# Per-layer embedding by whole fp32 products: weights loaded once, as they are

## The chip, the cores and the metric

The kernel runs on one core of one Trainium2 chip. The metric is the time of one execution in microseconds on the device; for the kernel before, three runs gave a median of 3856.39 us (3851.83 to 3856.41). Profiles and traces are of one further execution.

The engines are named as the profile names them: PE is TensorE (matmuls; PEld its weight loads), DVE is VectorE, ACT is ScalarE, POOL is GpSimd, SP is SyncE, which here only issues DMAs.

## The reference

One layer on 1024 tokens of width 1024, in fp32. What matters here is its end: the product-key experts and the per-layer input embedding.

```python
x = x + peer_ffn(rms_norm(x, norm_ffn[i]), peer_w_q[i], peer_sub_keys[i], peer_u[i], peer_v[i])
x = x + jax.nn.sigmoid(rms_norm(x, norm_ple[i]) @ ple_w_gate[i]) * (p[i] @ ple_w_proj[i])
return rms_norm(x, norm_final)
```

`peer_ffn` selects for every token 8 x 16 = 128 of 16384 experts, each a row `u` and a row `v` of 1024. The token's gates are multiplied by `gelu(h . u)` of the selected rows, and the sum of the `v` rows with these factors is added to x. The embedding multiplies the normed x (1024 wide) by `ple_w_gate` (1024 x 1024) and the input p (256 wide) by `ple_w_proj` (256 x 1024).

## The kernel before

The 1024 tokens are eight blocks of 128, one token per partition. The first part of the kernel (projections, time mixing, attention, selection of experts) takes some 2540 us and is not touched. What follows runs in overlap:

- `gather` (L895 to L909), for each block: the block's normed input is loaded by SP into one buffer, `gh` (L900); 128 times POOL gathers one `u` row per token by an indirect DMA (L904) and the DVE multiplies it with gh and sums it (L906). The rows have seven buffers, shared with `add_rows`. At 2543 us blocks 6 and 7 are still to be gathered, and the selection of the last blocks (L828 to L880, small DVE operations) is not finished.
- `dense` (L972 to L1006), for blocks 0 to 4: the sum over all experts. The factors, spread over all 16384 experts, lie in DRAM as W. SP loads pieces of W (`wr`, L986) and of v (`vr`, L996), both whole fp32. ACT writes a rounded copy as fp32r, the high half (L280), and the DVE the rest, the low half (L282). TensorE multiplies high by high, high by low and low by high (L1000 to L1002), and the DVE adds each finished bank to x (L1005).
- `add_rows` (L912 to L922), for blocks 5, 6 and 7: POOL gathers `v` rows (L919) and the DVE adds each with its factor (L921). Block 7's x lies in the buffer `gh`, so that its rows read `gh<-u,gate,gh`. They are the last rows of the kernel, and 93 of these 128 follow after the dense sum's last add.
- `ple_weights` and `ple`: the per-layer embedding and the final norm of all eight blocks, in the order 0 to 7. For a block, p and the normed x (`h`, L1042) are transposed by TensorE (L252), copied to SBUF by ACT as fp32r high halves (L257 for h, L255 for p), and the DVE makes low halves (L263, L261). The gate product has 8 steps over k for each of two halves n of the columns, the product with p 2 steps: 20 products of 128 x 128 by 128 x 512 a block, each as three fp32r matmuls (L292 to L294). ACT takes the sigmoid (L1052), the DVE multiplies (L1055), adds to x (L1057) and, after a norm, scales by gf (L1059); SP stores (L1060).
- `ple_weights` splits the weights in the same manner: each slice of 128 x 512 is loaded into one of two buffers `raw` (L1019), ACT makes the high half (L280), the low half is made by the DVE and POOL by turns (L282). Eight slices (w_pg, n = 0) lie in the right-hand pool and are loaded while the dense sum runs; the other twelve (w_pg, n = 1, and w_pp) are put into the left-hand pool, into the room that the dense sum leaves, and so come after it.

The order on each engine is set when the program is built: the instructions are placed by a simulated timeline and by priorities (`everything`, its list of steps with a number each; a smaller number goes first). On the chip each engine then works through its instructions in that order and waits on semaphores. SP's queue holds all direct loads and stores, the weights among them, in that order too.

## Time and profile before

| | before |
|---|---|
| median of 3 runs | 3856.39 us |
| profiled execution | 3855.49 us |
| its span (first to last instruction) | 3853.7 us |
| mean granted TensorE clock | 0.888 of full speed |
| busy over the span: PE, DVE, ACT, POOL | 81%, 81%, 32%, 48% |
| opening of the dense sum | 2543 to 2660 us |
| main part of it | 2660 to 3560 us |
| last add of the dense sum (L1005) to the end of the last row (L921) | 3634.3 to 3816.4 us |
| tail (rest of blocks 6 and 7) | 3816.4 to 3853.7 us |

The profile tells for every instruction when it ran, on which engine and by which line of the code, and what ended the idle time before it. An engine with a busy share near 100% in a stretch bounds that stretch if its work is needed there; a share over the whole span says little, since stretches differ. The granted clock is TensorE's, 1.0 being 2.4 GHz and 0.5 being 1.2 GHz. A matmul row's duration is longer than its share of the engine, since matmuls overlap: the step from one start to the next is what one costs. The same holds, by less, for the DVE.

### The profile page before, as it was taken

The page shows a single profiled execution, that of the slowest core. Times are in us where ns is not written, and L with a number is a line of the kernel's source. Part 1 is how long each engine was busy: PE and PEld are TensorE (multiplying, and loading weights), DVE is VectorE, ACT ScalarE, POOL GpSimd, SP SyncE. Part 2 cuts the span into 40 slices and gives each one's busy share as a digit, 9 for nine tenths or more (in the row PEclk, how much of TensorE's full clock was granted, in tenths as well). Part 3 has the DMA queues.
Part 4 walks back from the last instruction along what each step waited for, and adds up shares of the span by engine and source line. Part 5 has one row for each costly group of instructions (what it writes and reads, how often), then busy time and mean ns, then how long its engine had stood idle before and what let it go on. Part 6 is the DMA issues. An engine that isn't in the chain of part 4 may idle for free.

```text
span 3853.7 us, 61140 instructions
## 1 busy us (share of the span) xinstructions
PE 3104.5 (81%) x21615; PEld 2506.3 (65%) x21615; DVE 3110.8 (81%) x7003; ACT 1243.0 (32%) x2682; POOL 1856.3 (48%) x1494
## 2 busy tenths in 40 slices
PE   8998778787978686797866789648888989899767
PEld 7885777775667574577734567536666767677645
DVE  2532788767798786789878868989989999999997
ACT  3221322143121175212126866722222222222233
POOL 0000455544534553553455423346766766666772
PEclk9998899898989796898977789769999999989988
DMA  6236598899979898997988999889999999999984
GB/s 204 88 116 197 169 336 306 302 306 302 335 238 345 294 311 289 311 339 265 334 276 281 306 323 338 295 308 350 382 358 386 378 383 362 375 372 364 347 314 158
DMA packets 502322, 1160.41 MB, mean 301 GB/s; under 512 B 54016, under 2 KB 228352, under 8 KB 502016
## 3 DMA queue, kind: packets, MB, share of 16 engines
q0 software_dynamic: 202752, 738.29, 53.8%
q1 hardware_dynamic: 281984, 402.48, 30.6%
q10 hardware_dynamic: 17280, 15.74, 1.2%
q8 instruction: 171, 2.80, 0.3%
q14 instruction: 135, 1.11, 0.1%
HBM read 1071.38 MB, written 84.93 MB: 300 GB/s over the span
## 4 chain that ended last, share of the span: by engine, by line
PE 25%; DVE 23%; issue 20%; DMA 17%; POOL 9%; ACT 4%; SPq 1%; POOLq 0%; DVEq 0%; ACTq 0%; another core or an unknown queue 0%
DMA u<-in_u_dram,idx 9%; PE mm L290 9%; DVE u L906 8%; POOL u L904 6%; POOL u L919 3%; PE mm L785 2%; PE acc L1001 2%; DVE oa L963 2%; PE acc L1002 1%; DVE gh L921 1%; PE acc L1000 1%; DMA gate<-zT 1%; DMA raw<-zT 1%; PE w L965 1%; DVE x L921 1%
## 5 line engine op out<-in xcount | busy, mean ns | idle before, releaser
L904 POOL DMA_INDIRECT u<-in_u_dram,idx x1024 | 1248.3, 1219 | 1284.3 <-DVE dots L906 681.8
L906 DVE CUSTOM_DVE_ANT_0 u<-u,gh 128x1024 f32<-128x1024 f32 x1024 | 1249.9, 1233 | 220.0 <-DMA u<-in_u_dram,idx 201.8
L919 POOL DMA_INDIRECT u<-in_v_dram,idx x384 | 493.2, 1284 | 246.9 <-DVE x L921 116.4
L1001 PE MATMUL acc<-vlo,Whi 128*128 128x512 f32 x1280 | 529.2, 413 | 74.8 <-DVE vlo L282 73.0
L290 PE MATMUL mm<-hT,w 128*128 128x128 f32 x4608 | 561.4, 282 | 11.5 <-DMA w<-in_w_in_dram 2.3
L290 PEld LDWEIGHTS mm<-hT,w 128*128 128x128 f32 x4608 | 544.7, 197 | 27.7 <-issue 8.8
L1002 PE MATMUL acc<-vhi,Wlo 128*128 128x512 f32 x1280 | 521.1, 407 | 0.0
L1000 PE MATMUL acc<-vhi,Whi 128*128 128x512 f32 x1280 | 373.6, 404 | 90.8 <-DMA vr<-in_v_dram 38.9
L1000 PEld LDWEIGHTS acc<-vhi,Whi 128*128 128x128 f32 x1280 | 247.2, 194 | 167.0 <-ACT vhi L280 84.4
L1001 PEld LDWEIGHTS acc<-vlo,Whi 128*128 128x128 f32 x1280 | 253.0, 198 | 154.3 <-DVE vlo L282 99.1
L290 PE MATMUL mm<-act,w 128*128 128x256 f32 x1280 | 313.6, 399 | 33.5 <-DVE gate L776 14.6
L921 DVE SCALAR_TENSOR_TENSOR x<-u,gate,x 128x1024 f32<-128x1024 f32 x256 | 328.2, 1282 | 8.8 <-DMA u<-in_v_dram,idx 4.6
L280 ACT ACTIVATE vhi<-vr 128x512 fp32r<-128x512 f32 x256 | 158.3, 628 | 513.5 <-DMA vr<-in_v_dram 354.6
L965 PE MATMUL w<-ob,oa 128*128 128x128 f32 x1280 | 221.7, 330 | 96.0 <-ACT ob L959 62.5
L290 PEld LDWEIGHTS mm<-act,w 128*128 128x128 f32 x1280 | 247.8, 200 | 73.8 <-issue 16.9
L1002 PEld LDWEIGHTS acc<-vhi,Wlo 128*128 128x128 f32 x1280 | 253.6, 198 | 53.1
L965 PEld LDWEIGHTS w<-ob,oa 128*128 128x128 f32 x1280 | 202.2, 237 | 120.5 <-ACT ob L959 81.7
L963 DVE TENSOR_SCALAR oa<-cst,pt 128x128 f32<-128x128 f32 x640 | 190.2, 354 | 47.4 <-PE w L965 44.0
L958 ACT ACTIVATE ob<-cst,pt 128x128 f32<-128x128 f32 x640 | 204.0, 394 | 0.1
L280 ACT ACTIVATE Whi<-wr 128x1280 fp32r<-128x1280 f32 x64 | 81.4, 1274 | 313.0 <-PE acc L1001 276.3
L282 DVE TENSOR_TENSOR vlo<-vr,vhi 128x512 fp32r<-128x512 f32 x256 | 175.3, 697 | 5.1 <-ACT vhi L280 5.1
L921 DVE SCALAR_TENSOR_TENSOR gh<-u,gate,gh 128x1024 f32<-128x1024 f32 x128 | 169.9, 1327 | 1.0
(331 smaller groups left out, 4673.7 us busy)
## 6 DMA issues: line engine op xcount, KB each, us to landing
w<-in_w_in_dram SPq DMA_DIRECT2D x144, 512.0 KB
vr<-in_v_dram SPq DMA_DIRECT2D x256, 256.0 KB
W<-ws SPq DMA_DIRECT2D x40, 1024.0 KB
wr<-W SPq DMA_DIRECT2D x64, 640.0 KB
w<-in_w_q_dram SPq DMA_DIRECT2D x64, 512.0 KB
w<-in_w_out_dram SPq DMA_DIRECT2D x32, 512.0 KB
u<-in_u_dram,idx POOLq DMA_INDIRECT x1024
x<-in_x_dram SPq DMA_DIRECT2D x16, 512.0 KB
```

What stands on the lines that cost most here:

```text
L280: self.nc.scalar.activation(act[0], x, AF.Copy)
L290: mm(ps, w[0][:, i], a[0][:, i], start=first, stop=last)
L904: nc.gpsimd.indirect_dma_start(out=u[:], out_offset=None, in_=self.I["u"], in_offset=bass.IndirectOffsetOnAxis(ap=idx[:, k:k + 1], axis=0))
L906: nc.vector.tensor_tensor_reduce(out=u[:], in0=u[:], in1=h[:], scale=1.0, scalar=0.0, op0=OP.mult, op1=OP.add, accum_out=dots[:, k:k + 1])
L919: nc.gpsimd.indirect_dma_start(out=v[:], out_offset=None, in_=self.I["v"], in_offset=bass.IndirectOffsetOnAxis(ap=idx[:, k:k + 1], axis=0))
L921: nc.vector.scalar_tensor_tensor(x, v, gate[:, k:k + 1], x, op0=OP.mult, op1=OP.add)
L958: nc.scalar.activation(c[:, i], self.c("iota"), AF.Abs, bias=pt[:, 1, k + i:k + i + 1])
L963: nc.vector.tensor_scalar(a, self.c("iota"), pt[:, 0, k:k + 1], pt[:, 2, k:k + 1], op0=OP.is_equal, op1=OP.mult)
L965: nc.tensor.matmul(ps[:, i], a, c[:, i], start=True, stop=True)
L1000: nc.tensor.matmul(acc[b], wh, vh, start=i == 0, stop=False)
L1001: nc.tensor.matmul(acc[b], wh, vl, start=False, stop=False)
L1002: nc.tensor.matmul(acc[b], wl, vh, start=False, stop=i == G - 1)
```

## The change

All weights of the embedding are loaded as they are, in fp32, by two DMAs: w_pg (1024 x 1024, 4.19 MB) and w_pp (256 x 1024, 1.05 MB), both into the right-hand pool. The splits of the weights are gone, the second call of `ple_weights` too. Of h and p, ACT makes one whole fp32 copy after the transposes; their low halves are gone. `mm` is not changed: given one part of each factor it issues one matmul per product (L290), and given fp32 on both sides TensorE multiplies whole fp32. Before, an operand was given as two fp32r parts (`R` in the code), now as one fp32 part (`F`).

```diff
-    def ple_weights(self, n, side):
-
-        nc = self.nc
+    def ple_weights(self, side):
         pool = self.pool(self.ctx, "pw", side)
-        if n == 0:
-            self.raw = pool
-        for name, k, n in ([("w_pg", 8, 0)] if n == 0 else [("w_pg", 8, 1), ("w_pp", 2, 0), ("w_pp", 2, 1)]):
-            w = [self.tile(pool, [128, k, 512], R, f"{name}{n}{x}", 1) for x in ("hi", "lo")]
-            for i in range(k):
-                raw = self.tile(self.raw, [128, 512], F, "raw", 2)
-                nc.sync.dma_start(raw, self.I[name][i * 128:i * 128 + 128, n * 512:n * 512 + 512])
-                self.split_to([x[:, i] for x in w], raw, nc.gpsimd if i % 2 else nc.vector)
-            self.pw[name, n] = w
+        for name, k in (("w_pg", 8), ("w_pp", 2)):
+            w = self.tile(pool, [128, k, D], F, name, 1)
+            self.nc.sync.dma_start(w, self.I[name].rearrange("(k p) n -> p k n", p=128))
+            for n in range(2):
+                self.pw[name, n] = (w[:, :, n * 512:n * 512 + 512],)
 ...
-            pair = lambda k, tag: [t([128, k, 128], tag + x, HB, R) for x in ("hi", "lo")]
+            whole = lambda k, tag: [t([128, k, 128], tag + "T", HB)]
 ...
-                hT, pT = pair(8, "h"), pair(2, "p")
+                hT, pT = whole(8, "h"), whole(2, "p")
 ...
-            (59, self.ple_weights, 1), (60, self.ple, range(8)),
+            (60, self.ple, range(8)),
```

Line numbers behind L1010 are smaller by six in the changed kernel: its sigmoid is L1046, the multiplication and the add on the DVE are L1049 and L1051, the last scaling L1053, the store L1054; the two weight loads are L1013.

The change moves instructions at three places. The first is SP's queue at the opening of the dense sum, after the first two wr and three vr. Before:

```order
L996 DMA vr_23258<-in_v_dram 128x512
L1019 DMA raw_22354<-in_w_pg_dram 128x512
L1019 DMA raw_22358<-in_w_pg_dram 128x512
L900 DMA gh_22393<-h_6_289_357 128x1024
L986 DMA wr_23199<-W_0_291_359 128x1280
L986 DMA wr_23205<-W_0_291_359 128x1280
L996 DMA vr_23279<-in_v_dram 128x512
L996 DMA vr_23300<-in_v_dram 128x512
L996 DMA vr_23321<-in_v_dram 128x512
L1019 DMA raw_22362<-in_w_pg_dram 128x512
```

and now:

```order
L996 DMA vr_23228<-in_v_dram 128x512
L1013 DMA w_pg_22352<-in_w_pg_dram 128x8x1024
L1013 DMA w_pp_22354<-in_w_pp_dram 128x2x1024
L900 DMA gh_22363<-h_6_289_357 128x1024
L986 DMA wr_23169<-W_0_291_359 128x1280
L986 DMA wr_23175<-W_0_291_359 128x1280
L996 DMA vr_23249<-in_v_dram 128x512
L996 DMA vr_23270<-in_v_dram 128x512
L996 DMA vr_23291<-in_v_dram 128x512
```

The two whole weights stand where the first two slices stood, ahead of gh and of the next wr and vr; the later slices are gone.

The second is the DVE at the same place, around its first rows of block 6's gather (L906, printed as ISA, the second of each pair reads out the sum). `eq` and `idf` are tiles of the last selection (L868, L870, L871). Before, the sixth and seventh row, and the splits behind them:

```order
L906 ISA u_5001_22414,dots_22395<-u_5001_22414,gh_22393 128x1024
L906 ISA dots_22395 128x1
L868 TENSOR_TENSOR eq_19256<-bp_19228,cst_60 128x640
L906 ISA u_4998_22405,dots_22395<-u_4998_22405,gh_22393 128x1024
L906 ISA dots_22395 128x1
L282 TENSOR_TENSOR Wlo_23202<-wr_23199,Whi_23201 128x10x2x64
L282 TENSOR_TENSOR Wlo_23208<-wr_23205,Whi_23207 128x10x2x64
L282 TENSOR_TENSOR vlo_23282<-vr_23279,vhi_23281 128x512
L282 TENSOR_TENSOR vlo_23303<-vr_23300,vhi_23302 128x512
L282 TENSOR_TENSOR vlo_23324<-vr_23321,vhi_23323 128x512
L870 TENSOR_TENSOR eq_19256<-eq_19256,ci_19206 128x640
```

and now, up to the first row:

```order
L871 TENSOR_REDUCE idf_19231<-eq_19260 128x2x8
L873 CAST idx_4046_19229<-idf_19231 128x64
L868 TENSOR_TENSOR eq_19275<-bp_19228,cst_60 128x800
L870 TENSOR_TENSOR eq_19275<-eq_19275,ci_19206 128x800
L871 TENSOR_REDUCE idf_19231<-eq_19275 128x2x8
L868 TENSOR_TENSOR eq_19289<-bp_19228,cst_60 128x640
L870 TENSOR_TENSOR eq_19289<-eq_19289,ci_19206 128x640
L871 TENSOR_REDUCE idf_19231<-eq_19289 128x4x8
L868 TENSOR_TENSOR eq_19293<-bp_19228,cst_60 128x800
L870 TENSOR_TENSOR eq_19293<-eq_19293,ci_19206 128x800
L871 TENSOR_REDUCE idf_19231<-eq_19293 128x2x8
L906 ISA u_22366,dots_22365<-u_22366,gh_22363 128x1024
```

Five groups of the selection that stood among and behind the first rows (from eq_19256 on) now all stand ahead of the first row.

The third is the DVE at the last rows of block 7 (gh_30041 before, gh_30011 now), where sg and x are those of block 6. Before, from the last row on:

```order
L921 SCALAR_TENSOR_TENSOR gh_30041<-u_30424,gate_4047_19230,gh_30041 128x1024
L261 TENSOR_TENSOR plo_31433<-tr_31434,phi_31432 128x128
L232 TENSOR_SCALAR nms_31445<-nss_31442 128x1
L261 TENSOR_TENSOR plo_31433<-tr_31438,phi_31432 128x128
L1055 TENSOR_TENSOR sg_31513<-sg_31513,mm_31515 128x512
L217 RECIPROCAL nrsy_31447<-nrst_31448 128x1
L1057 TENSOR_TENSOR x_6509_29655<-x_6509_29655,sg_31513 128x512
L218 SCALAR_TENSOR_TENSOR nrst_31448<-nrsy_31447 128x1
L1055 TENSOR_TENSOR sg_31549<-sg_31549,mm_31551 128x512
L219 TENSOR_TENSOR nrst_31448<-nrst_31448,nms_31445 128x1
L1057 TENSOR_TENSOR x_6509_29655<-x_6509_29655,sg_31549 128x512
```

and now, up to the last row:

```order
L921 SCALAR_TENSOR_TENSOR gh_30011<-u_30370,gate_4047_19230,gh_30011 128x1024
L1051 TENSOR_TENSOR x_6501_29625<-x_6501_29625,sg_31074 128x512
L921 SCALAR_TENSOR_TENSOR gh_30011<-u_30373,gate_4047_19230,gh_30011 128x1024
L1049 TENSOR_TENSOR sg_31090<-sg_31090,mm_31092 128x512
L921 SCALAR_TENSOR_TENSOR gh_30011<-u_6752_30376,gate_4047_19230,gh_30011 128x1024
L1051 TENSOR_TENSOR x_6501_29625<-x_6501_29625,sg_31090 128x512
L921 SCALAR_TENSOR_TENSOR gh_30011<-u_6753_30379,gate_4047_19230,gh_30011 128x1024
L921 SCALAR_TENSOR_TENSOR gh_30011<-u_6754_30382,gate_4047_19230,gh_30011 128x1024
L921 SCALAR_TENSOR_TENSOR gh_30011<-u_6755_30385,gate_4047_19230,gh_30011 128x1024
L921 SCALAR_TENSOR_TENSOR gh_30011<-u_30388,gate_4047_19230,gh_30011 128x1024
L921 SCALAR_TENSOR_TENSOR gh_30011<-u_30391,gate_4047_19230,gh_30011 128x1024
L921 SCALAR_TENSOR_TENSOR gh_30011<-u_30394,gate_4047_19230,gh_30011 128x1024
```

Block 6's multiplications and adds stood behind the last row; now the first of them stands right ahead of the rows shown, the other three among these, and six rows follow after the last.

## Rows read from the trace of the kernel before

**Rows 1.** Busy time of each engine by stretch (start:end of the stretch in us, its length, busy us and number of instructions of PE, PEld, DVE, ACT and POOL, granted TensorE clock, busy share of the DMA engines, GB/s): the opening of the dense sum, its main part, and the stretch from its last add to the last row added.

```profile
2543.00:2660.00 117.00, 84.85 (x312) 64.62 (x313) 109.81 (x205) 30.57 (x41) 66.56 (x48) 0.85 0.91 325
2660.00:3560.00 900.00, 801.82 (x3233) 626.12 (x3233) 846.03 (x1080) 200.16 (x273) 611.62 (x464) 0.95 0.99 373
3634.30:3816.40 182.10, 123.53 (x480) 89.75 (x481) 172.80 (x273) 66.66 (x143) 118.38 (x92) 0.84 0.85 292
```

**Rows 2.** Groups of instructions by line and shape from 3634.3 to 3816.4 (line, engine, operation, out<-in, shapes, count | busy us, mean ns of one | idle us before them, and what ended most of it).

```profile
L921 DVE SCALAR_TENSOR_TENSOR gh<-u,gate,gh 128x1024 f32<-128x1024 f32 x93 | 125.1, 1345 | 0.5
L919 POOL DMA_INDIRECT u<-in_v_dram,idx x86 | 110.5, 1285 | 53.5 <-issue 14.8 <-DVE hlo L263 10.5 <-DVE gh L921 9.2
...
L263 DVE SCALAR_TENSOR_TENSOR hlo<-tr,vec,hhi 128x128 fp32r<-128x128 f32 x56 | 18.6, 343 | 1.1 <-ACT hhi L257 0.9
...
L282 POOL TENSOR_TENSOR w_pg1lo<-raw,w_pg1hi 128x512 fp32r<-128x512 f32 x4 | 5.1, 1280 | 0.1
...
L261 DVE TENSOR_TENSOR plo<-tr,phi 128x128 fp32r<-128x128 f32 x15 | 4.0, 283 | 0.0
```

**Rows 3.** The same view for the DVE from 2660 to 3560.

```profile
L921 DVE SCALAR_TENSOR_TENSOR x<-u,gate,x 128x1024 f32<-128x1024 f32 x252 | 323.1, 1282 | 8.7 <-DMA u<-in_v_dram,idx 4.6
...
L282 DVE TENSOR_TENSOR vlo<-vr,vhi 128x512 fp32r<-128x512 f32 x216 | 146.1, 688 | 3.0 <-ACT vhi L280 3.0
```

**Rows 4.** The DVE in order of time (start us, duration us, engine, line, operation, out<-in, shapes, count), around the first h of the per-layer embedding, and its last row update.

```profile
3643.58 0.75 DVE L1042 TENSOR_SCALAR h<-x,nrsy 128x1024 f32<-128x1024 f32 x1
...
3646.75 2.78 DVE L921 SCALAR_TENSOR_TENSOR gh<-u,gate,gh 128x1024 f32<-128x1024 f32 x1
3649.46 0.34 DVE L263 SCALAR_TENSOR_TENSOR hlo<-tr,vec,hhi 128x128 fp32r<-128x128 f32 x1
3649.72 1.27 DVE L921 SCALAR_TENSOR_TENSOR gh<-u,gate,gh 128x1024 f32<-128x1024 f32 x1
...
3815.16 1.28 DVE L921 SCALAR_TENSOR_TENSOR gh<-u,gate,gh 128x1024 f32<-128x1024 f32 x1
```

**Rows 5.** TensorE in order of time, one k-step of block 7's gate product, columns as in rows 4.

```profile
3832.21 0.27 PE L252 MATMUL tr<-cst,h 128*128 128x128 f32 x1
...
3833.01 0.39 PE L293 MATMUL mm<-w_pg0lo,hhi 128*128 128x512 f32 x1
3833.24 0.39 PE L292 MATMUL mm<-w_pg1hi,hhi 128*128 128x512 f32 x1
...
3833.71 0.27 PE L252 MATMUL tr<-cst,h 128*128 128x128 f32 x1
```

**Rows 6.** L785, the product with w_out: all its matmul records (duration in ns: least, median, most; first and last start), then two rows of TensorE's timeline there, columns as in rows 4. `tr` and `mm` are names of the banks that the products go to.

```profile
L785 PE MATMUL mm<-w,act x192: 592/592/1222, 336.3 to 2322.1; 128*128 128x512 f32 x192
...
L785 PE MATMUL tr<-w,act x64: 592/592/877, 337.2 to 2323.0; 128*128 128x512 f32 x64
...
338.05 2.74 PE L785 MATMUL mm<-w,act 128*128 128x512 f32 x6
340.62 1.02 PE L785 MATMUL tr<-w,act 128*128 128x512 f32 x2
```

**Rows 7.** SP (first row, the start of its next loads), POOL (second row) and the DVE in order of time at the opening of the dense sum, columns as in rows 4, in brackets the idle us before an instruction and what ended it.

```profile
2542.90 0.81 SPq L986 DMA_DIRECT2D wr<-W  x2
...
2552.94 1.73 POOL L282 TENSOR_TENSOR w_pg0lo<-raw,w_pg0hi 128x512 fp32r<-128x512 f32 x1 [17.39 <-DMA gh<-h]
...
2558.65 0.98 DVE L868 TENSOR_TENSOR eq<-bp,cst 128x800 int16<-128x800 uint32 x1
...
2559.75 0.56 DVE L870 TENSOR_TENSOR eq<-eq,ci 128x800 int16<-128x800 int16 x1
...
2560.34 0.99 DVE L871 TENSOR_REDUCE idf<-eq 128x16 f32<-128x800 int16 x1
...
2561.45 1.22 DVE L906 CUSTOM_DVE_ANT_0 u<-u,gh 128x1024 f32<-128x1024 f32 x1
...
2590.91 0.69 DVE L282 TENSOR_TENSOR vlo<-vr,vhi 128x512 fp32r<-128x512 f32 x1 [0.79 <-ACT vhi L280]
2592.86 0.69 DVE L282 TENSOR_TENSOR vlo<-vr,vhi 128x512 fp32r<-128x512 f32 x1 [1.26 <-ACT vhi L280]
...
2595.51 2.31 DVE L906 CUSTOM_DVE_ANT_0 u<-u,gh 128x1024 f32<-128x1024 f32 x1
...
2608.31 2.77 DVE L906 CUSTOM_DVE_ANT_0 u<-u,gh 128x1024 f32<-128x1024 f32 x1
```

**Rows 8.** The tail in order of time, ACT and DVE, columns as in rows 7.

```profile
3817.87 1.28 ACT L1052 ACT_TABLE_LOAD   x1
...
3819.16 1.09 ACT L1052 ACTIVATE sg<-mm 128x512 f32<-128x512 f32 x2
...
3824.05 0.75 DVE L1042 TENSOR_SCALAR h<-gh,nrsy 128x1024 f32<-128x1024 f32 x1
...
3841.51 1.09 ACT L1052 ACTIVATE sg<-mm 128x512 f32<-128x512 f32 x2 [1.34 <-PE mm L294]
```

**Rows 9.** TensorE in order of time at the start of block 6's products, columns as in rows 7.

```profile
3800.77 0.69 PE L252 MATMUL tr<-cst,h 128*128 128x128 f32 x2 [4.59 <-DVE h L1042]
...
3802.72 0.63 PE L292 MATMUL mm<-w_pp0hi,phi 128*128 128x512 f32 x1
3803.15 0.63 PE L293 MATMUL mm<-w_pp0lo,phi 128*128 128x512 f32 x1
```

More of the change, by code (lines that the diff above doesn't have):

```diff
@@ L1106, in everything @@
                 elif f == self.ple_weights:
-                    f(a, ("right", "left")[a])
+                    f("right")
                 else:
```

## The prediction

> **What bounds the kernel now.** Read first the busy time by stretch [rows 1]. Of 3853.7 us of span the change touches three stretches: the opening of the sum over all experts (2543 to 2660), where the weight slices of the first half are loaded and split; the stretch from the end of that sum's last add (L1005, 3634.3) to the end of the last gathered row (L921, begun 3815.16 [rows 4]), called stage B, 182.1 us; and the tail behind it, 37.3 us. The 900 us between contain none of this work. In stage B the DVE is busy 172.8 of 182.1 us (95%), TensorE 123.5, POOL 118.4, the DMA engines 85%. So read next what the DVE does there, by groups [rows 2]: 93 row updates (L921) of 1345 ns hold 125.1 us, and behind them come the low halves of the activations (L263, L261) and of the weights. The same row update takes 1282 ns in the dense stretch, where POOL splits nothing [rows 3]. The DVE's timeline [rows 4] gives the steps from one start to the next, which is what an instruction costs in a full queue: 0.08 us less than its own length, since so much of it lies under the next. Stage B is bound by the DVE, with TensorE second; the opening is bound by the DVE too (109.8 of 117 us) [rows 1].
>
> **The change part by part.** All sums go against the profiled execution, 3855.49 us, span and 1.8 us around it; the median of the three runs is 0.9 higher, which I neglect.
>
> *DVE in stage B.* Removed: 56 low halves of h at 0.26 (3649.46 to 3649.72 [rows 4]), 14.6 us; 15 of p at 0.283 - 0.08, 3.0 us [rows 2]; six weight splits (every other one of the twelve slices that are split here), shaped as vlo, at 0.69 - 0.08, 3.7 us [rows 3]. The POOL splits go as well. While one ran, an L921 took 2.78 us in place of 1.27 [rows 4], so I charge them the difference of the two means, 93 x (1345 - 1282) = 5.9 us [rows 2, 3]. Together 27.2. Added before the last row: block 6's four adds, which stood behind it (the DVE rows of the order above), 4 x 0.60 = 2.4 us. With its 9.3 us of idle time kept the DVE needs 182.1 - 27.2 + 2.4 = 157.3 us.
>
> On the pair of POOL and DVE the Trainium skill, SBUF — State Buffer (section "SBUF: two separate sides"), says that a DVE operation with two SBUF inputs and a GpSimd operation that reads SBUF take the shared port pair whole, one after the other. The row of 2.78 us, which is 1.27 and some 1.5 of waiting, agrees. By the rule alone each of stage B's six POOL splits could cost at least its 1.28 us [rows 2], 7.7 in all, and the sum would be 1.8 us lower; I keep the 5.9 of the means.
>
> *TensorE in stage B.* A product was three fp32r matmuls, 0.23 us apart (3833.01 to 3833.24), 0.69 us; a k-step of two products and one transpose took 1.50 us (3832.21 to 3833.71), so a transpose is 0.13 [rows 5]. A whole fp32 product of the same size already stands in the kernel: L785 shows 256 records for its 128 products, and six records take 2.57 us (338.05 to 340.62), 0.428 each [rows 6]; so a product is 0.857 us. A block has 20 products and 10 transposes: 20 x 0.69 + 1.3 = 15.0 us before, 17.1 + 1.3 = 18.4 now. The change makes TensorE slower by 3.4 us a block; it is the price of the freed DVE. Counted from the start of stage B: the first h is done at 10.0 (3643.58 + 0.75 [rows 4]); block 0's 17.1 and 3 us for a start at the low clock (as in the tail, below) give 30.1; six more blocks 110.4; then, since the four adds of block 6 now precede the last rows, 2.4 us of adds and nine rows of 1.28: 154.4. That is at 2.4 GHz throughout. With the granted clock of 0.95 that the dense stretch had [rows 1], the 127.5 us of products grow by 6.7, to a total of 161; with stage B's present 0.84 by 24, to 176 with the first block's 3 us counted once.
>
> Two chains in program order, 157 on the DVE and 161 on TensorE, that hand h and sigmoid to each other: I take 163, two for the hand-overs, and keep 157 and 176 as ends. TensorE will be busier than now, so its clock should stand nearer to 0.95 than to 0.84. Neither POOL's 86 gathers (110.5 us and the 14.8 of issue between them, 125 [rows 2]) nor the bytes (292 GB/s x 182.1 = 53.2 MB, less 2.6 MB for ten slices of weights, at 373 GB/s 136 us [rows 1]) reach 157. Term: -19.
>
> *Opening.* Removed on the DVE: four weight splits at 0.61, 2.4 us; the slowing of two instructions beside POOL's splits, L906 of 2.31 and 2.77 for 1.22, 2.6 us; two waits of 0.79 and 1.26 for late vr, 2.1, since SP stood before these at raw slices with only two buffers [rows 7]: 7.1 in all. Added: the whole weights, 5.24 MB, stand in SP's queue ahead of gh (the SP rows of the order above). Ahead of and with gh there were 3.15 MB, and it landed when POOL's wait for it ended, 2552.94 [rows 7]; now there are 7.86 MB from 2542.9. At the 373 GB/s of the dense stretch that is 21.1 us, at the opening's 325 [rows 1] 24.2: gh lands between 2564 and 2567. Its first reader, L906, began at 2561.45. But the DVE's order is another one too: five groups of the last selection (L868, L870, L871), which stood among and behind the first L906, now stand before them. One group of 800 columns takes 0.98 + 0.56 + 0.99 less 3 x 0.08, 2.3 us [rows 7]; three of these and two of 640 columns, 1.8 each, are 10.5, and the first L906 is due near 2571, with gh there. So the wait for gh costs the DVE nothing; if this cover failed, it would be 3 to 6 us. Two things are late next. The second wr and vr stand behind gh, 2.1 MB or 5.6 us, so by 2573, and their splits come after seven L906, 8 us from 2571: hidden. POOL's gathers, held by seven row buffers, go on at 2571 and not at 2563, with 2.62 MB more to move before the sum's end. At 373 GB/s these bytes are 7.0 us, and the DMA share in the dense stretch is 0.99; but the DVE is busy for 846 of its 900 us [rows 1], so I charge half, 3.5. Term: -7.1 + 3.5, -4 rounded; bounds -9 (the bytes hidden, more splits slowed by POOL than the two) and +10 (first rival).
>
> *Loads and room.* The right-hand pool now holds whole weights, 40 KB a partition. The ten slices of stage B are gone from SP, and with them TensorE's waits for them, which lay beside the full DVE and earn nothing by themselves.
>
> *Tail.* Block 7's h was made 7.6 us after the last row (3824.05 against 3816.44), partly because block 6's table load and two sigmoids (1.28 + 1.09) stood on ACT in between; these now precede: -2.4. From h (3824.80) to the sigmoid (3841.51) TensorE took 16.7 us: 54 matmuls at 0.23, 12.4, eight transposes 1.1, and so about 3.2 of low clock. Now 18 x 0.857 + 1.1 + 3.2 = 19.7: +3.0. The last two products of w_pp, 1.71 for 1.37: +0.3 [rows 8]. Term +1, bounds -2 and +4.
>
> Sum: -4 - 19 + 1 = -22, so 3855.5 - 22 = **3834 us** (rounded up). With the ends of the three terms, not all at once, the forecast's own range is 3820 to 3850.
>
> **Rivals.**
> First, the transfers bind the opening and the sum: the 7.1 us freed on the DVE there turn into waits, the 2.62 MB cost their 7.0, and some 3 more go with the gathers that stop until 2571: opening +10, and 3855.5 + 10 - 19 + 1 = 3848. For: a DMA share of 0.91 and 0.99 [rows 1]. Against: the DVE's 94% in the same stretch.
>
> Second, rows limit stage B whatever the DVE is freed of, by the arrival of the gathers: it stays at 182, opening and tail -4 and +1, some 3853, or 3857 where the opening gives nothing. For: a DMA share of 0.85. Against: only 0.5 us of idle time stand before those 93 L921 [rows 2].
>
> Third, the other side: TensorE becomes the bound and falls to the low clock at every block. Where h came late, it sat idle for 4.59 us before the transposes at 3800.77, and its matmuls then were 0.43 apart (3802.72 to 3803.15), the 1.2 GHz level, in place of 0.23 [rows 9]. If every block keeps this, a cycle is 18.4 + 4.6 + 3 = 26.0; stage B 30.1 + 6 x 26 + 13.9 = 200, +18, and the time 3855.5 - 4 + 18 + 1 = 3871. It decides from a cycle of 23.4, where stage B is 184. For: the granted clock in stage B is 0.84, below the sum's 0.95; there is one buffer for h. Against: h came late because the DVE was full, and it gets 27 us back. The Trainium skill, TensorE: Matmul & The Clock Gate (section "HAM oscillation — how this bites in real kernels"), describes such a loop of waits and cold starts; the row at 3800.77 bears it out for one block.
>
> **How the numbers follow.** A measurement of this kernel tells 0.2%, 7.7 us, from no change: faster is below 3848.7, slower above 3864.1. Chances: forecast 0.70, transfers 0.12 (at the border, half of it faster, half the same), rows 0.06 (same), TensorE 0.12 (slower). Faster 0.76, same 0.12, slower 0.12. The range 3820 to 3858 takes in the first two rivals and leaves out the third and a rest below.
>
> **What would show it.** Right: stage B near 163 with L921's mean near 1282; on TensorE a cycle of 18 to 21 us a block, each product 0.857; the first L906 of the opening near 2571, without a wait for gh, and nothing but gathers on POOL. Wrong: a stage B of 180 or more with idle DVE time before the adds of sigmoid (third rival) or before L921 (second); products at 1.7 us through most of a block; a first L906 later than 2575, or waits for gathered rows (L906, L921) in the sum well above those of before; or a whole product that takes longer here than L785's.

## The result and the profile after

| | before | changed |
|---|---|---|
| median of 9 runs | 3851.83 us | 3828.17 us |
| lowest, highest | 3844.08, 3857.55 us | 3809.59, 3845.54 us |
| ratio, 95% interval | | 0.9936 [0.9919, 0.9953] |
| profiled execution, its span | 3855.49, 3853.7 us | 3822.98, 3821.0 us |

The ratio is 24.7 us less (0.0064 x 3851.83; by its interval 18 to 31). The forecast was 22 us less, 3834 us.

The profile is read in the same stretches as before. The first view is the busy time by stretch of the changed kernel, columns as in [rows 1]: the opening (from the first wr of the sum, 2536.49), stage B (from the end of the sum's last add, 3627.81, to the end of the last row, 3784.63), the tail, two pieces out of the middle of stage B, then its first 12 us, its stretch from 3640 to 3772, and its last 12 us.

```profile
2536.49:2653.49 117.00, 82.88 (x320) 64.29 (x320) 105.32 (x202) 27.32 (x35) 60.91 (x45) 0.83 0.92 353
3627.81:3784.63 156.82, 133.16 (x352) 58.97 (x352) 148.08 (x199) 62.69 (x135) 110.82 (x87) 0.94 0.91 323
3784.63:3821.00 36.37, 20.50 (x48) 8.80 (x48) 8.00 (x22) 11.82 (x22) 0.00 (x0) 0.78 0.07 29
...
3660.00:3680.00 20.00, 19.66 (x54) 8.80 (x53) 19.50 (x30) 9.18 (x20) 14.73 (x12) 1.00 0.93 325
...
3740.00:3760.00 20.00, 18.79 (x52) 8.30 (x51) 18.57 (x29) 10.63 (x23) 15.56 (x12) 1.00 0.91 312
...
3627.80:3640.00 12.20, 4.88 (x9) 2.19 (x10) 11.95 (x21) 3.00 (x8) 8.44 (x8) 0.50 0.93 318
3640.00:3772.00 132.00, 127.67 (x343) 56.78 (x342) 123.69 (x169) 59.70 (x127) 97.36 (x78) 1.00 0.93 330
3772.60:3784.60 12.00, 0.01 (x1) 0.00 (x0) 11.82 (x12) 0.00 (x0) 4.43 (x3) 0.70 0.65 253
```

These answer to [rows 1]. Stage B has shrunk from 182.1 to 156.8 us with the DVE at 94% again (148.1 of 156.8), and TensorE, at 133.2, is now busy for 19.66 of 20 us in a middle piece, with the full clock granted. From the first load to the last add of the sum it is 1091.3 us, where it was 1091.5 (2542.90 to 3634.36). The tail is 36.4 us after 37.3. So of the 26.3 us between the two profiles behind the first load, 25.3 are stage B's. The first load itself comes 6.4 us earlier, which has to do with nothing that was changed: the same instructions stand ahead of it in both kernels, and in the fourteen profiles of this study it lies anywhere between 2528 and 2557. Much of the spread of the times above probably comes from there (only one execution of each run was profiled), and so the stretches are compared behind that point.

Next the groups of the DVE in stage B, columns as in [rows 2]:

```profile
L921 DVE SCALAR_TENSOR_TENSOR gh<-u,gate,gh 128x1024 f32<-128x1024 f32 x93 | 119.1, 1280 | 0.8
L1051 DVE TENSOR_TENSOR x<-x,sg 128x512 f32<-128x512 f32 x14 | 9.6, 683 | 0.0
L1049 DVE TENSOR_TENSOR sg<-sg,mm 128x512 f32<-128x512 f32 x14 | 9.5, 680 | 0.3 <-ACT sg L1046 0.3
...
L1036 DVE TENSOR_SCALAR h<-x,nrsy 128x1024 f32<-128x1024 f32 x7 | 5.2, 747 | 1.4 <-PE tr L252 1.4
```

The same 93 row updates take 1280 ns in place of 1345. L263, L261 and the weight splits of [rows 2] are gone. In all the DVE's busy time fell by 24.7 us (172.8 to 148.1), and it stands idle for 8.7 us after 9.3. The adds are 14 and not 12, since block 6's now precede the last row.

### The profile page after: what moved, and what is told of

Same layout as the page of the kernel before. It is cut to its first block, busy times and chain, and to the rows that moved or that the text cites. A ratio compares the mean times of both kernels' runs of the same rounds, so it can differ in the third digit from the quotient of the medians.

```text
span 3821.0 us, 60686 instructions
## 1 busy us (share of the span) xinstructions
PE 3108.5 (81%) x21455; PEld 2473.7 (65%) x21455; DVE 3070.8 (80%) x6913; ACT 1232.2 (32%) x2662; POOL 1821.1 (48%) x1484
## 3 DMA queue, kind: packets, MB, share of 16 engines
q1 hardware_dynamic: 280416, 402.48, 30.7%
## 5 line engine op out<-in xcount | busy, mean ns | idle before, releaser
L904 POOL DMA_INDIRECT u<-in_u_dram,idx x1024 | 1224.4, 1196 | 1318.8 <-DVE dots L906 720.1
L906 DVE CUSTOM_DVE_ANT_0 u<-u,gh 128x1024 f32<-128x1024 f32 x1024 | 1243.3, 1226 | 220.5 <-DMA u<-in_u_dram,idx 215.2
L290 PE MATMUL mm<-hT,w 128*128 128x128 f32 x4608 | 566.6, 284 | 11.0 <-ACT z L326 2.9
L290 PEld LDWEIGHTS mm<-hT,w 128*128 128x128 f32 x4608 | 550.4, 199 | 27.1 <-ACT z L326 6.5
L290 PE MATMUL mm<-act,w 128*128 128x256 f32 x1280 | 314.4, 401 | 28.2 <-DMA act<-yg 9.6
L921 DVE SCALAR_TENSOR_TENSOR x<-u,gate,x 128x1024 f32<-128x1024 f32 x256 | 328.1, 1282 | 7.1 <-DMA u<-in_v_dram,idx 2.9
L290 PEld LDWEIGHTS mm<-act,w 128*128 128x128 f32 x1280 | 250.0, 201 | 67.9 <-issue 12.0
L921 DVE SCALAR_TENSOR_TENSOR gh<-u,gate,gh 128x1024 f32<-128x1024 f32 x128 | 163.9, 1281 | 1.3
```

Of the source, the lines that this page charges most:

```text
L290: mm(ps, w[0][:, i], a[0][:, i], start=first, stop=last)
L904: nc.gpsimd.indirect_dma_start(out=u[:], out_offset=None, in_=self.I["u"], in_offset=bass.IndirectOffsetOnAxis(ap=idx[:, k:k + 1], axis=0))
L906: nc.vector.tensor_tensor_reduce(out=u[:], in0=u[:], in1=h[:], scale=1.0, scalar=0.0, op0=OP.mult, op1=OP.add, accum_out=dots[:, k:k + 1])
L921: nc.vector.scalar_tensor_tensor(x, v, gate[:, k:k + 1], x, op0=OP.mult, op1=OP.add)
```

## Experiments

All kernels are read in the same stretches, in profiles of one execution each; "rows" are the L921 that follow the sum's last add, since the order on the DVE sometimes moves a few of them (1.28 us each) across that line. The last column is the ratio to the kernel before. "Half" stands for the twelve slices (3.1 of the 5.24 MB) that came after the sum in the kernel before. The changed kernel, e1, e2 and e4 have the same instructions in opening and sum, and their six profiles lie between 1086.4 and 1095.1 there (mean 1090.6); e3 and e8, alike there but for loads in the last 3 us, differ by 7.1. A few us in that column show nothing by themselves.

| kernel | opening and sum | stage B (rows) | tail | first load to end | ratio, 95% interval |
|---|---|---|---|---|---|
| before | 1091.5 | 182.1 (93) | 37.3 | 1310.8 | |
| changed | 1091.3 | 156.8 (93) | 36.4 | 1284.5 | 0.9936 [0.9919, 0.9953] |
| changed, e9 | 1090.4 | 156.1 (93) | 36.1 | 1282.6 | 0.9939 [0.9918, 0.9961] |
| changed, e12 | 1086.4 | 156.1 (93) | 36.0 | 1278.5 | 0.9939 [0.9918, 0.996] |
| e1 low halves back | 1093.3 | 176.6 (93) | 37.8 | 1307.8 | 1.0 [0.9979, 1.0021] |
| e2 h on ACT | 1095.1 | 160.7 (93) | 36.3 | 1292.1 | 0.9954 [0.9932, 0.9977] |
| e3 half of the weights late | 1076.1 | 168.8 (92) | 36.4 | 1281.3 | 0.995 [0.9928, 0.9972] |
| e4 no product with w_pp | 1086.9 | 157.0 (93) | 34.9 | 1278.8 | 0.995 [0.9931, 0.9968] |
| e5 weights behind gh | 1089.4 | 156.0 (93) | 36.0 | 1281.4 | 0.9903 [0.987, 0.9937] |
| e6 before, no splits on POOL | 1097.4 | 170.1 (88) | 34.0 | 1301.5 | one run |
| e7 e5 with weights loaded twice | 1099.3 | 151.2 (90) | 36.2 | 1286.7 | 0.9952 [0.9935, 0.9969] |
| e8 e3 with p first | 1083.2 | 167.5 (92) | 37.4 | 1288.1 | 0.9962 [0.9946, 0.9978] |
| e10 half of the weights in the sum | 1089.2 | 145.4 (87) | 36.0 | 1270.6 | 0.9906 [0.9883, 0.9929] |
| e10 again, e11 | 1083.7 | 145.2 (87) | 35.8 | 1264.7 | 0.9917 [0.9901, 0.9934] |

**Is it the DVE's work?** e1 gives the DVE its low halves back and changes nothing else.

```diff
+                lo = t([128, 8, 128], "lo", HB, R)
-                self.to_T(part, [p], pT)
+                self.to_T(part, [p], pT + [lo])
-                self.to_T(part, [h], hT, "norm_ple")
+                self.to_T(part, [h], hT + [lo], "norm_ple")
```

> The changed kernel, with the low halves of h and p computed again on the DVE, into a tile that nothing reads. In the changed kernel the stretch from the last L1005 to the last L921 (stage B) took 156.8 us, DVE busy 148.1, TensorE 133.2 at a cycle of 19 us a block. Theory (the DVE's freed work is the gain): 56 x 0.26 + 14 x 0.20 = 17.4 us come back on the DVE, whose floor is then 165.5; stage B 166 to 172, the time 9 to 15 us above the changed kernel's. Rival (the gain came from weights that lie ready, not from the DVE): stage B stays at 157 within 2.

Measured: 176.6 us of stage B, 19.8 above the changed kernel, and a ratio of 1.0: the whole gain is gone again. Stage B and the two groups, in the views of above:

```profile
3643.63:3820.27 176.64, 145.88 (x352) 63.01 (x352) 164.16 (x271) 60.66 (x135) 116.98 (x87) 0.93 0.84 288
```

```profile
L921 DVE SCALAR_TENSOR_TENSOR gh<-u,gate,gh 128x1024 f32<-128x1024 f32 x93 | 118.8, 1277 | 0.5
L263 DVE SCALAR_TENSOR_TENSOR lo<-tr,vec,hT 128x128 fp32r<-128x128 f32 x56 | 18.0, 342 | 4.6 <-ACT hT L257 4.6
```

The rows keep their 1277 ns, so it is the low halves themselves. They cost 2.4 us more than the 17.4 counted: the DVE is busy for 16.1 us more and idle for 3.7 more, with 4.6 us of waits for ACT's copies (second row). TensorE waited 16.8 us for these copies too, likely since a transpose's bank is now held until the DVE has read it; that was not tried apart. What is left to 182.1, 5.5 us, is all that weights without splits are worth while the DVE is full otherwise and TensorE has the whole products.

**TensorE or the DVE?** e4 takes four of 20 products from each block. It leaves out the product with w_pp and multiplies the sigmoid by the gate's own bank, so that the DVE's work stays.

```diff
-                    ps = bank([128, 512])
-                    self.mm(ps, pT, wp, 2)
                     nc.vector.tensor_tensor(sg, sg, ps, op=OP.mult)
```

> The changed kernel without the product with w_pp: the sigmoid is multiplied by the gate's own bank instead, so the DVE's work stays and TensorE loses 4 of 20 products a block, 3.4 us. Theory (two chains of about the same length): TensorE's cycle falls from 19 to below 16 and the DVE alone holds stage B, with 148 busy and a few us at its ends: 150 to 153. Rival (the DVE alone holds it already): 156 to 157.

Measured: 157.0 us.

```profile
3632.56:3789.53 156.97, 110.73 (x296) 48.66 (x296) 149.10 (x199) 62.71 (x135) 105.44 (x87) 0.87 0.91 324
```

TensorE is busy for 110.7 us in place of 133.2, the DVE for 149.1, and the stage is as long as in the changed kernel. The rival is right: TensorE's 3.4 us a block are worth nothing in stage B. e2 goes the other way and takes the making of h from the DVE.

```diff
-                nc.vector.tensor_scalar(h, x, rs, None, op0=OP.mult)
+                nc.scalar.activation(h, x, AF.Copy, scale=rs)
```

> The changed kernel with h = x * rstd on ACT in place of the DVE. Theory (stage B is held by two chains, the DVE 94% busy and TensorE 98% busy from 3640 to 3770): 7 x 0.67 = 4.7 us leave the DVE, TensorE's 5.4 us of waits for h shrink; stage B 152 to 155, tail +0.3, the time 2 to 5 us below the changed kernel's. Rival (TensorE alone binds by its products): stage B 156 to 158, no gain. Second rival (ACT's longer instruction, some 1.05 us for 0.75, puts h later): stage B 158 to 160.

Measured: 160.7 us, 4 more, just above the second rival's range, and the theory's 2 to 5 us less are refuted. The DVE has less to do (144.5 us busy, after 148.1) and idles more. The view of its waits in stage B, of e2 and then of the changed kernel (in total us, times, longest):

```profile
DVE sg L1049 <- ACT sg L1046: 9.3, 6, 6.3
DVE sg L1049 <- PE mm L290: 1.4, 1, 1.4
```

```profile
DVE frsy L217 <- ACT frst L216: 4.7, 6, 1.3
DVE h L1036 <- PE tr L252: 1.4, 1, 1.4
DVE sg L1049 <- ACT sg L1046: 0.3, 1, 0.3
```

The rows behind a multiplication of the sigmoid (L1049) stand in the DVE's order, so a sigmoid that comes later holds them up: 9.3 us of such waits in place of 0.3. Here a step taken off the full engine and put on the chain that feeds it did not pay.

**Do POOL's splits stretch the rows?** e6 is the kernel before, with every low half of the weights on the DVE.

```diff
-                self.split_to([x[:, i] for x in w], raw, nc.gpsimd if i % 2 else nc.vector)
+                self.split_to([x[:, i] for x in w], raw, nc.vector)
```

> The kernel before, with the low halves of all weights made by the DVE, none by POOL. In the kernel before 93 L921 of stage B took 1345 ns each, in the changed kernel 1280. Theory (POOL's splits stop the DVE's two-input instructions): the mean falls to 1282 or below without any other change, stage B loses 5.9 us and gains 6 x 0.61 = 3.7 on the DVE: 179 to 181. Rival (the longer L921 come from the loads of slices or from ACT's high halves, not from POOL): the mean stays at 1335 or above and stage B is 185 to 187.

The group of rows in its stage B:

```profile
L921 DVE SCALAR_TENSOR_TENSOR gh<-u,gate,gh 128x1024 f32<-128x1024 f32 x88 | 112.5, 1279 | 0.4
```

1279 ns, with the slices and ACT's high halves as before: it was POOL. Stage B lasts 170.1 us with five rows fewer in it, so 176.5 with the same number: 5.6 us less than before, where 1 to 3 were expected. In the kernel before, the first of the six POOL splits met a split of the DVE, which took 1.35 us in place of 0.69 [rows 3], and the other five each met one row. These are that split and the longest of the rows:

```profile
3634.27 1.35 DVE L282 TENSOR_TENSOR w_pg1lo<-raw,w_pg1hi 128x512 fp32r<-128x512 f32 x1
...
3658.65 2.87 DVE L921 SCALAR_TENSOR_TENSOR gh<-u,gate,gh 128x1024 f32<-128x1024 f32 x1
```

So the rows and this split explain 2.9 us (5.9 and 0.7 won, 3.7 of splits added); the other 2.7 of this one execution stay open. The five rows that stage B lacks in e6 stand in the sum, which is 1097.4 - 6.4 = 1091.0 without them, unchanged.

**What do the early loads cost?** e3 has the whole products, but brings only 2.1 of the 5.24 MB early.

```diff
+        for name, k, n in ([("w_pg", 8, 0)] if n == 0 else [("w_pg", 8, 1), ("w_pp", 2, 0), ("w_pp", 2, 1)]):
+            w = self.tile(pool, [128, k, 512], F, f"{name}{n}", 1)
+            for i in range(k):
+                self.nc.sync.dma_start(w[:, i], self.I[name][i * 128:i * 128 + 128, n * 512:n * 512 + 512])
...
+            (59, self.ple_weights, 1), (60, self.ple, range(8)),
```

> Whole fp32 products as in the changed kernel, but the weights loaded at the times of before: w_pg n=0 in eight slices at the opening, the other twelve slices after the sum into the left-hand pool, without splits. Theory (DVE work is the gain; the added bytes ate the opening's): stage B 157 to 164 (block 0 may wait up to 7 us for 3.1 MB of late slices), opening and sum together 1086 to 1089 us where both kernels had 1091. Rival (the weights' early arrival is the gain): stage B 172 to 182.

Measured: 1076.1 us of opening and sum, 13 less than the mean of the three profiles of the changed kernel (1089.4), more than the theory asked for, and 168.8 of stage B, 12 more, also outside of its range. The second has a likely reason in the timeline: TensorE stood idle for 27.5 us before the first transposes of p, which had been loaded behind the late slices in SP's queue (the view puts the end of the wait down to a row).

```profile
3642.40 0.66 PE L252 MATMUL tr<-cst,p 128*128 128x128 f32 x2 [27.45 <-DVE gh L921]
```

e8 puts gf and the first p ahead of the late slices (`(61, self.ple_weights, 1)` in place of 59).

> The kernel of e3 (half of the weights late, without splits) with gf and the first two p loaded ahead of the late slices: in e3 TensorE stood idle for 27.5 us at the start of stage B because p lay behind 3.1 MB. Theory (bytes out of the sum are worth some 8 us and more, and only p's place spoilt stage B): opening and sum 1074 to 1084, stage B 158 to 164, since the n=1 products of block 0 still wait for their slices; in all 10 us below the changed kernel, ratio to the kernel before near 0.991. Rival (e3's 1076 was luck, or the late slices stop the gathers as much as they freed): opening and sum 1086 to 1093, or stage B above 167; no gain over the changed kernel.

Measured: 1083.2 and 167.5 us, and from the first load to the end 1288.1, no gain.

```profile
3628.75 0.66 PE L252 MATMUL tr<-cst,p 128*128 128x128 f32 x2 [8.95 <-DMA w_pg<-in_w_pg_dram]
...
3645.07 2.08 PE L290 MATMUL mm<-w_pp,pT 128*128 128x512 f32 x2 [5.33 <-DMA w_pp<-in_w_pp_dram]
```

```profile
3656.20 0.69 DVE L1049 TENSOR_TENSOR sg<-sg,mm 128x512 f32<-128x512 f32 x1 [11.02 <-ACT sg L1046]
```

The order of the queue was not all: p is there early now, but block 0's products wait for w_pp, and the DVE for the sigmoid. Late slices are late, whichever lies first.

Two kernels look at the opening by itself. e5 holds the whole weights back until gh is there (the step `ple_weights` of the list in `everything` is gone for it), and e7 loads them twice (the line with `range(2)` is e7's alone; in e5 the two lines under it stand once).

```diff
+            self.gh = h
+            if b == 6:
+                self.ple_weights("right")
...
+            for _ in range(2):
+                self.nc.scalar.activation(w[:, 0, :1], self.gh[:, :1], AF.Copy)
                 self.nc.sync.dma_start(w, self.I[name].rearrange("(k p) n -> p k n", p=128))
```

> The changed kernel with its two weight loads held back until gh has landed (each waits for a copy of one column of gh by ACT), so that SP issues gh and the next wr and vr ahead of the 5.24 MB. Opening and sum together took 1091.5 us before, 1091.3 in the changed kernel and 1076.1 where only half of the weights came early. Theory (the 15 us are 7 us for 2.62 MB more in a stretch held by the DMA engines, and some 8 us for which they stood still, since gh and with it the first L906 came 12 us later): gh comes on time, the first L906 18 to 22 us after the first load, opening and sum 1080 to 1086. Rival (the bytes alone, wherever they are put ahead of the sum's end): 1088 to 1093. Stage B as in the changed kernel, 155 to 159.

> The kernel of e5 (weights after gh) with each of the two weight loads issued twice, so that 5.24 MB more stand in SP's queue behind gh. Theory after e5 (the stretch is held by the bytes: late gh cost next to nothing, e5's opening and sum were 1089.4): 5.24 / 0.373 = 14 us more, 1100 to 1107, half of it at the least; stage B and tail unchanged. Rival (the bytes are hidden beside the DVE, and e3's 15 us came from something else): 1086 to 1094.

In e5 the first L906 comes 17.4 us after the first load, where it came 30.7 after it in the changed kernel, and opening and sum are 1089.4, exactly the changed kernel's mean. The rival is right within the spread: the late gh cost nothing that lasts to the sum's end. The ratio of e5, 0.9903 from five runs, is lower than the changed kernel's, with intervals that overlap; its stretches show no gain. In e7 the second load of 5.24 MB makes 1286.7 us out of 1281.4 from the first load to the end (the sum is 9.9 longer, with three rows more in it): 5.3 us, a third of the 14 that the bytes alone would take, 1.0 us for each MB. Neither the theory nor its rival had that; it lies between them. But the three profiles of the changed kernel differ by 6.0 us in this stretch, so that it takes an earlier point to see the price.

Such a point is the sum's tenth add of 160, the last of its first group, at which every kernel but e5 (38) has done 36 rows of block 6. These rows end with it, in the kernel before, the changed one, e7, e10 (the kernel below) and e11 (e10 again), whose first loads start at 2542.9, 2536.5, 2528.4, 2556.6 and 2551.4:

```profile
2643.36 0.68 DVE L1005 TENSOR_TENSOR x<-x,acc 128x512 f32<-128x512 f32 x1
...
2633.57 1.28 DVE L1005 TENSOR_TENSOR x<-x,acc 128x512 f32<-128x512 f32 x2
...
2633.03 1.27 DVE L1008 TENSOR_TENSOR x<-x,acc 128x512 f32<-128x512 f32 x2
...
2647.68 3.08 DVE L1005 TENSOR_TENSOR x<-x,acc 128x512 f32<-128x512 f32 x5
...
2642.19 3.07 DVE L1005 TENSOR_TENSOR x<-x,acc 128x512 f32<-128x512 f32 x5
```

From the first load it ends at 101.1 us before, at 98.0 to 99.4 in the six profiles of the changed order, at 99.2 in e5, at 105.9 in e7, and at 93.9 to 94.9 in e3, e8, e10 and e11. So 5.24 MB more cost 6.7 us here (e7 against e5), or some 9 if e5's two rows more are counted, and 3.1 MB less save 4.4 in the mean: 1.3 to 1.7 us for each MB. Part of the 4.4 may come from the earlier first L906 of these four, 23 us after the first load.

e10 draws on both: 2.1 MB at the opening, the rest inside the sum, each piece behind one of its later groups (`g` counts from 0, so these are the eleventh, twelfth and thirteenth of 16). The weights get a tile of their own for each piece; that part of the edit is left out here.

```diff
+                if g in (10, 11, 12):
+                    self.load(*(("w_pg", 1), ("w_pp", 0), ("w_pp", 1))[g - 10], xs[0][:, :1])
```

> The changed kernel with its weights in four pieces, all in the right-hand pool: w_pg n=0 at the opening as in e3, the other 3.1 MB inside the sum, each after the sum's tenth, eleventh and twelfth of 16 groups (a copy of one column by ACT holds each load back). The opening then carries 2.1 MB in place of 5.24, and p and the gathers of stage B meet no weights. Theory (from e3, e8: 8 to 15 us less in opening and sum with half of the weights out of them; from e7: 1 us for each MB put back into the sum): opening and sum 1080 to 1088, stage B 155 to 158, tail 36 to 37; from the first load to the end 1272 to 1282 where the changed kernel had 1282.6 and 1284.5. Rival (the bytes cost the same wherever in the sum they stand, and e3 gained by moving them out of it altogether): opening and sum 1089 to 1093, no gain.

> The kernel of e10 unaltered, beside the changed kernel on the same chip. From the first load to the end e10 took 1270.6 us, the changed kernel 1284.5 and 1282.6. Theory (that gain is the kernel's): 1268 to 1275 again, and a ratio to the kernel before that lies 0.002 to 0.004 under the changed kernel's. Rival (it was one execution's): 1280 or more.

> The changed kernel unaltered, beside e7 and e8, to see how far its stretches repeat. Its one profile had opening and sum 1091.3 us, stage B 156.8, tail 36.4; kernels with the same order there had 1093.3, 1095.1 and 1086.9 for the first. Expected: 1087 to 1096, stage B 155 to 159, tail 36 to 37; the start of the opening may lie anywhere between 2533 and 2552, as it did in the runs so far, which no change behind it can cause.

> The changed kernel a third time, for the comparison with e11: opening and sum 1089 to 1093, stage B 155 to 158, tail 36 to 37, 1281 to 1286 from the first load to the end.

e10's opening and stage B, and the changed kernel's in e12, which ran beside e11:

```profile
2556.60:2673.60 117.00, 84.95 (x344) 66.60 (x345) 108.95 (x212) 27.45 (x35) 63.69 (x48) 0.89 0.91 341
3645.80:3791.24 145.44, 132.80 (x352) 58.84 (x352) 140.32 (x193) 61.95 (x135) 99.91 (x80) 0.96 0.90 326
```

```profile
2542.60:2659.60 117.00, 82.57 (x320) 63.26 (x320) 105.44 (x202) 27.24 (x35) 62.90 (x45) 0.84 0.93 354
3629.01:3785.08 156.07, 132.45 (x352) 58.70 (x352) 148.04 (x199) 62.68 (x135) 108.64 (x87) 0.94 0.91 326
```

From the first load to the end e10 and e11 take 1270.6 and 1264.7 us, the changed kernel 1284.5, 1282.6 and 1278.5. By the stretches that is 14 us less; the ratios, 0.9906 and 0.9917 against 0.9936 and twice 0.9939, say 7 to 13, with intervals that overlap. As read, e10's opening and sum (1089.2) lie in its rival's range and stage B lies below the forecast one; six rows had moved from the one into the other, which nobody had forecast. With these put back, the sum gained 8 to 13 us and stage B some 3. e10 has the shortest time behind the first load of this study, and e11 lies below its own range; by the ratio e5 is no slower. The three profiles of the changed kernel repeat stage B and tail within 0.7 us, opening and sum within 5; e12's 1086.4 and 1278.5 lie below the ranges named for it.

## Why the prediction was right, point by point

**The bound and the DVE's sum: right.** Stage B was the DVE's, and its working gave 182.1 - 27.2 + 2.4 = 157.3 us; 156.8, 156.1 and 156.1 were measured. The parts hold too: the DVE's busy time fell by 24.7 us, where 27.2 less 2.4 were worked out; the row update went from 1345 to 1280 ns, 6.0 us for 93 where 5.9 were charged, and e6 shows that POOL's splits did it; the low halves cost 19.8 us when put back (e1), where 17.6 were taken off. By the rule of the Trainium skill, SBUF — State Buffer (section "SBUF: two separate sides"), that the one of such a pair that starts first holds the shared ports for its whole instruction, each split could have cost its 1.28 us, 7.7 in all. The trace nearly agrees: five splits met a row each and made it 0.9 to 1.6 us longer, 6.3 together, and the sixth made a split of the DVE 0.7 longer.

**TensorE: the price of a product was right, its weight in the sum was not.** A whole product costs two records of 0.43 us here as in [rows 6], and the cycle of a block is 19 us, within the 18 to 21 named:

```profile
3642.24 0.27 PE L252 MATMUL tr<-cst,h 128*128 128x128 f32 x1
3642.35 1.88 PE L290 MATMUL mm<-w_pg,hT 128*128 128x512 f32 x4
3644.07 0.27 PE L252 MATMUL tr<-cst,h 128*128 128x128 f32 x1
...
3655.04 0.38 PE L252 MATMUL tr<-cst,h 128*128 128x128 f32 x2
3655.76 1.99 PE L290 MATMUL mm<-w_pp,pT 128*128 128x512 f32 x4 [0.34 <-ACT sg L1046]
...
3673.93 0.38 PE L252 MATMUL tr<-cst,h 128*128 128x128 f32 x2
3674.65 1.98 PE L290 MATMUL mm<-w_pp,pT 128*128 128x512 f32 x4 [0.34 <-ACT sg L1046]
...
3770.62 1.98 PE L290 MATMUL mm<-w_pp,pT 128*128 128x512 f32 x4 [0.56 <-ACT sg L1046]
3790.19 0.69 PE L252 MATMUL tr<-cst,h 128*128 128x128 f32 x2 [17.58 <-DVE h L1036]
```

Four records take 1.72 us (3642.35 to 3644.07), and from block 0's last products (3655.76) to block 1's (3674.65) it is 18.9 us. The mean clock rose to 0.94, near to the 0.95 taken. What failed is the step "Two chains in program order, 157 on the DVE and 161 on TensorE, that hand h and sigmoid to each other: I take 163, two for the hand-overs". In the 161 stood 6.7 us for a clock of 0.95 in all products. But the clock was at 0.50 in the first 12 us of stage B, for which 3 us stood in the sum already, and at 1.00 from 3640 to 3772, while products ran. Block 6's products end 144.8 us into stage B, where the 161 had 147. And nothing was to be added for the hand-overs: after block 6's products TensorE waits for 17.6 us, for block 7's h, while the DVE still has adds and rows to do. e4 shows it: TensorE could lose 3.4 us a block, and stage B stayed at 157. The term was -25 to -26 and not -19.

**Opening: somewhat too hopeful, within its bounds.** -4 was forecast. At the sum's last add -0.2, -1.1 and -5.1 are measured against the one profile of before, and with profiles that differ so much the size is not known there. At the tenth add it is clearer: 98.0 to 99.4 us after 101.1, so some -2 to -3. e10 and e11, whose opening carries 2.1 MB of weights (2.6 before), are 6.9 and 7.2 us ahead of the kernel before, about the 7.1 that was to be freed on the DVE; the changed kernel keeps a third of it. The cover was as forecast: the five selection groups stand before the first L906, which begins without waiting for gh (30.7 us after the first load; 28 were named; when gh landed no row shows), and POOL stands still until then:

```profile
2566.31 0.99 DVE L871 TENSOR_REDUCE idf<-eq 128x16 f32<-128x800 int16 x1
2567.22 1.22 DVE L906 CUSTOM_DVE_ANT_0 u<-u,gh 128x1024 f32<-128x1024 f32 x1
```

```profile
2568.71 1.68 POOL L904 DMA_INDIRECT u<-in_u_dram,idx  x1 [39.95 <-DVE dots L906]
```

Up to the sum's end the DVE's freed time went into other waits. Its busy time there is 5.9 us shorter (1027.3 to 1021.4) and its idle time 5.8 us longer (64.2 to 69.9). These are the two largest waits from the first load to the last add, before and after:

```profile
DVE Wlo L282 <- ACT Whi L280: 23.0, 17, 10.3
DVE u L906 <- DMA u<-in_u_dram,idx: 17.1, 24, 2.5
```

```profile
DVE Wlo L282 <- ACT Whi L280: 29.1, 16, 11.9
DVE u L906 <- DMA u<-in_u_dram,idx: 20.6, 27, 2.6
```

They grew by 9.6 us, and the smaller ones shrank by 3.8. For the 2.62 MB more, 3.5 us were charged, half of their transfer; by the price at the tenth add, 1.3 to 1.7 us for each MB, it is 3.4 to 4.5. Of the 8 to 13 us that e10 and e11 win in opening and sum over the whole load, 4 to 5 are there at the tenth add. The rest is not explained by bytes, since e10 moves the same bytes within the sum; it is also no larger than the spread between equal kernels there. The same two waits are 39.0 us in e10, 34.4 in e11 and 33.7 in e3, against 46.3 to 49.7 in the changed kernel and 46.0 in e5, but in e10 and e11 others grew. Where the rest comes from was not tried apart and stays open.

**Tail: sign wrong, size small.** +1 was forecast, -0.9 to -1.3 came. Block 7's h came 4.8 us after the last row (5.2 forecast), and from h to the second sigmoid it took 19.0 (19.7 forecast; 16.7 before, to the first of two that follow at once [rows 8]):

```profile
3784.72 1.06 ACT L230 ACTIVATE eq<-gh 128x1024 bf16<-128x1024 f32 x1 [13.66 <-DVE gh L921]
...
3789.38 0.75 DVE L1036 TENSOR_SCALAR h<-gh,nrsy 128x1024 f32<-128x1024 f32 x1
...
3808.30 0.60 ACT L1046 ACTIVATE sg<-mm 128x512 f32<-128x512 f32 x1 [2.63 <-PE mm L290]
3809.16 0.60 ACT L1046 ACTIVATE sg<-mm 128x512 f32<-128x512 f32 x1 [0.26 <-PE mm L290]
```

From there to the end it is 11.8 us, where 12.2 + 0.3 were taken. Each of the three was taken a little too long.

**The rivals.** Transfers: they took back some of the opening's gain, 2 of the 14 us that lie between the forecast's -4 and the rival's +10. Rows: refuted, stage B fell to 156.8 us, with 0.8 us of idle time before the 93 rows. TensorE falling to the low clock at every block: refuted, the granted clock is 1.00 from 3640 to 3772, through blocks 1 to 6; it is low in the first 12 us, and falls again after block 6's products, when TensorE is idle.

Of the sum -4 - 19 + 1 = -22, stage B gave 6 us more, the tail 2 more and the opening 2 less. By the stretches the change is worth 26 to 32 us, by the ratio 24.7 (18 to 31): 22 was near, and short by the one step on TensorE; that it was so near is in part the opening, whose miss went the other way.

## What to carry to other kernels

Where one engine is full in a stretch, add up its own queue by steps from one start to the next, keep the idle time that it had, and take that as the stretch's length. Here a second engine that was nearly full added nothing, as its chain ended before the first one's, and a step moved from the full engine onto the chain that feeds it cost more than it freed. Whole fp32 products cost TensorE a quarter more than three fp32r ones here (0.86 against 0.69 us), and are the better choice where the engine that makes the halves is the full one. Prefetching all of a weight at the head of a busy stretch was not free: 1.3 to 1.7 us for each MB by the first group's end. Loaded in pieces, the rest behind later groups, the same weights cost less here.

## What the runs showed beyond that

The first load of the sum lay between 2528.4 and 2556.6 us in fourteen profiles of kernels that differ only behind that point, while stage B and tail of one kernel repeat within 1 us. So a difference of 10 us between the whole times of two single executions says nothing about a late stage; the stage's own stretch in one profile each says it at once.

A split on POOL of 1.28 us made single two-input instructions of the DVE up to 1.6 us longer (L921 of 2.87 us above; [rows 4, 7]), and without POOL's splits none of the groups of rows has a mean above 1282 ns.
